# A channel mixer's first projection as seven half-size products per gate/up pair, from un-normalised sums, with the product kept in DRAM

## The chip, the cores and the metric

The kernel runs on one core of a Trainium2 chip, as one program in one launch. The metric is the device time of the launch in microseconds (us); a kernel's time is the median of its runs. A profiled execution is a single run with the hardware profiler; it gives the trace and its page.

## The reference, cut to what matters

One layer of a hybrid encoder works on 1056 frames of 1024 channels in float32: 1024 frames of a prompt and 32 of a sample stream, each group with its own modulation vectors. The token mixer (gated linear attention beside a short convolution) comes first, then the channel mixer:

```python
x = x + g1 * (merged @ w_o)                       # merged: 1024 channels
h = rmsnorm(x, norm2_g) * (1 + sc2) + sh2
gt, upv = jnp.split(h @ w_ffn_in, 2, axis=-1)     # 1024 -> 2 x 2816
x = x + g2 * ((jax.nn.silu(gt) * upv) @ w_ffn_out)
y = rmsnorm(x, norm_f_g)
```

## The kernel before, in words

Everything is kept transposed: channels on the 128 partitions, frames along the free axis. T = 1056 frames are cut into three blocks of 384, 384 and 288 columns (BO). A float32 product is three matmuls in the rounded format fp32r: every operand is split into a high part (a cast on ACT) and a low part (operand minus high part), and hi·hi, hi·lo and lo·hi are added up in PSUM (gemm_block). Weights come through load_w: one DMA of 512 KB on SP's queue into one of two raw buffers, a cast of 128x1024 on ACT, and a subtraction of 128x1024 on POOL.

The program is one list of steps, written in an order by hand; a scheduler then fixes each engine's instruction order, and each engine runs its list strictly in order. The stages are, by the trace:

- 0 to about 300 us: the first norm, the modulation vectors, q, k and v.
- to about 600 us: the attention, filled up with the projections of the convolution.
- to about 1010 us: output gate, merge gates, the attention's output projection.
- to about 1208 us: w_conv_out (loop over 8 weights, 3 blocks each), then w_o in three passes, one for each block, so that each of its 8 weights is loaded three times. The residual sum x1 stays in SBUF. Squares are summed on DVE (sq_acc), inv_rms turns them into 1/rms with a product with ones, a square root on ACT and RECIPROCAL on DVE, and norm2 writes the normalised, shifted and split operand h2.
- to the end: the channel mixer, in four parts of 5, 5, 6 and 6 of the 22 gate/up pairs (PARTS). For a pair, gemm2 takes for each block 24 matmuls of the gate's weight and 24 of the up weight, 144 in all; ev_gt applies silu on ACT, ev_up multiplies on DVE, and split makes the operand `a` of the second projection, its low part on POOL. After each part, w_ffn_out is applied to these `a` and added to x1 (add_gated).

A pair's inner work is thus this, once per block:

```python
gemm_block(psa, wa, acta, b, list(range(KT)))
t = eva(b, psa[:, : wd(b)])
psb = psm.tile([P, 512], F32, tag="m", name=nm("ps"))
gemm_block(psb, wb, actb, b, list(range(KT)))
evb(b, psb[:, : wd(b)], t)
```

Of the kernel before, what the change touches and what calls it, by code (L numbers as in the profile page):

```python
# [7 lines left out]
F32 = mybir.dt.float32  # L8
# [5 lines left out]
P = 128  # L14
# [18 lines left out]
PARTS = (5, 5, 6, 6)  # L33
# [24 lines left out]
def segs(b):  # L58
    lo, hi = BO[b], BO[b + 1]
    if hi <= S:  # L60
        return [(lo, hi, 0)]
    return [(lo, S, 0), (S, hi, 1)]
# [3 lines left out]
def hybrid_trunk(  # L66
# [117 lines left out]
    # ================= input norm, modulation, q/k/decay/v =================  # L184
    with tc.tile_pool(name="p1", bufs=1) as p1:
# [343 lines left out]
    # ================= gated linear attention, with the conv projections =================  # L529
    with tc.tile_pool(name="gl", bufs=1) as gl:  # L530
# [378 lines left out]
    # ================= merge, output projection, channel mixer =================  # L909
# [6 lines left out]
    def bt(b, tag, bufs=2):  # L916
        return r2.tile([P, BW], F32, tag=tag, name=nm(tag), bufs=bufs)[:, : wd(b)]

    og = []
    for j in range(KT):  # L920
        hi, lo = big(2 * j), big(2 * j + 1)
        og.append((hi, lo))

        def ev_g(b, ps, j=j, hi=hi, lo=lo):
            o = bt(b, "o")
            nc.sync.dma_start(o, o_d[:, j, blk(b)])
            sg = bt(b, "t")
            nc.scalar.activation(sg, ps, AF.Silu)
            nc.vector.tensor_tensor(sg, sg, o, op=ALU.mult)
            split(sg, hi[:, blk(b)], lo[:, blk(b)], "act", "dve")  # L930

        gemm(load_w(w_in[G0 + j]), h, ev_g)

    def gemm2(wa, acta, eva, wb, actb, evb, hook=None):
        for b in range(NB):
            if hook is not None and b == NB - 1:
                hook()
            psa = psm.tile([P, 512], F32, tag="m", name=nm("ps"))
            gemm_block(psa, wa, acta, b, list(range(KT)))
            t = eva(b, psa[:, : wd(b)])  # L940
            psb = psm.tile([P, 512], F32, tag="m", name=nm("ps"))
            gemm_block(psb, wb, actb, b, list(range(KT)))
            evb(b, psb[:, : wd(b)], t)

    for j in range(KT):

        def ev_ga(b, ps):
            sa = bt(b, "sa")
            nc.scalar.activation(sa, ps, AF.Sigmoid)
            return sa  # L950

        def ev_ya(b, ps, sa, j=j):
            nc.vector.tensor_tensor(sa, ps, sa, op=ALU.mult)
            nc.scalar.dma_start(mg_d[j][:, blk(b)], sa)

        gemm2(load_w(w_in[GA0 + j]), h, ev_ga, load_w(w_gla_out[j]), og, ev_ya)

    cpair = []
    for j in range(KT):

        def ev_gb(b, ps, j=j):
            sb = bt(b, "sa")
# [253 lines left out]
```

## Time and profile before

| | |
|---|---|
| time, median of 3 runs | 2021.74 us (2021.61 to 2021.79) |
| profiled execution: span, first to last instruction | 2017.7 us |
| PE (TensorE) busy, matmuls | 1928.9 us, 12121 |
| DVE (VectorE), ACT (ScalarE), POOL (GpSimd) busy | 863.2, 575.6, 728.9 us |
| mean granted TensorE clock | 0.984 of full speed |

Some 4 us of the time lie around the profile's span. Busy time is a union: back-to-back matmuls overlap, so a matmul's own duration is longer than the distance from its start to the next one's start, and it is this distance (called pitch below) that counts for a PE without gaps.

### The profile page before, as it was taken

The numbers are of one execution on the slowest core, as the hardware profiler recorded it, in microseconds if no ns is written. First come the engines' busy times: TensorE is split into PE (matmuls) and PEld (weight loads), VectorE is DVE, ScalarE is ACT, GpSimd is POOL, SyncE is SP. The second block draws the span as 40 slices with busy tenths as digits, with TensorE's granted clock in tenths as the row PEclk, the third lists the DMA queues.
The fourth block names the chain that finished last, engine by engine and source line by source line (L and its number), as shares of the span: only waits on it lengthen the run. The fifth ranks groups of instructions, "written<-read, shape, count | busy, mean of one in ns | idle before, by whom it ended". The sixth has DMA issues, their size and how long they took to land.

```text
span 2017.7 us, 29207 instructions
## 1 busy us (share of the span) xinstructions
PE 1928.9 (96%) x12121; PEld 1906.5 (94%) x12121; DVE 863.2 (43%) x1275; ACT 575.6 (29%) x940; POOL 728.9 (36%) x457
## 2 busy tenths in 40 slices
PE   6699988999999999999999998999999999999997
PEld 5699888998999999999999998999999999999997
DVE  7999958787773441000015688002002100110036
ACT  5333444444431231111312245211211111112122
POOL 5732247667542221222521353422322333223330
PEclk9799999999999999999999999999999999999999
DMA  7576843233212321222534453112111111111112
GB/s 273 174 278 212 275 126 108 76 104 94 77 61 74 108 90 63 66 83 87 164 102 142 137 168 99 53 34 62 43 41 44 54 52 35 47 46 42 55 40 87
DMA packets 102006, 200.56 MB, mean 99 GB/s; under 512 B 13457, under 2 KB 64785, under 8 KB 101874
## 3 DMA queue, kind: packets, MB, share of 16 engines
q1 hardware_dynamic: 73394, 165.26, 25.9%
q10 hardware_dynamic: 28480, 33.44, 4.7%
q8 instruction: 95, 1.56, 0.3%
q14 instruction: 37, 0.30, 0.0%
HBM read 165.15 MB, written 33.51 MB: 98 GB/s over the span
## 4 chain that ended last, share of the span: by engine, by line
PE 76%; DVE 12%; issue 4%; DMA 3%; POOL 2%; ACT 2%; SPq 1%; DVEq 0%; ACTq 0%; POOLq 0%
PE ps L132 71%; DVE junk L218 3%; PE pso L132 1%; POOL dt L740 1%; PE psv L132 1%; PE psk L132 1%; DMA wm<-in_w_modT 1%; DVE o L1043 1%; DVE td L444 1%; DVE h L349 1%; DVE tt L745 1%; DVE tt L744 0%; ACT whi L136 0%; PE psn L132 0%; PE pslv L132 0%
## 5 line engine op out<-in xcount | busy, mean ns | idle before, releaser
L140 POOL TENSOR_TENSOR wlo<-raw,whi 128x1024 fp32r<-128x1024 f32 (+2 forms) x170 | 397.4, 2339 | 718.9 <-ACT whi L136 703.6
L132 PE MATMUL ps<-h,whi 128*128 128x384 f32 (+2 forms) x2496 | 600.4, 325 | 6.6 <-DVE vst L511 4.0
L132 PE MATMUL ps<-g,whi 128*128 128x384 f32 (+1 forms) x2352 | 563.0, 325 | 0.0
L132 PEld LDWEIGHTS ps<-h,whi 128*128 128x128 f32 x2496 | 438.0, 190 | 7.5 <-ACT ta L435 4.2
L132 PEld LDWEIGHTS ps<-g,whi 128*128 128x128 f32 x2352 | 410.4, 188 | 0.3
L132 PE MATMUL ps<-h,wlo 128*128 128x384 f32 (+2 forms) x1248 | 405.6, 325 | 1.9 <-POOL wlo L140 1.9
L132 PE MATMUL ps<-g,wlo 128*128 128x384 f32 (+1 forms) x1176 | 380.0, 323 | 1.6 <-POOL wlo L140 1.6
L136 ACT CAST whi<-raw 128x1024 fp32r<-128x1024 f32 (+2 forms) x172 | 172.9, 1005 | 455.9 <-PE ps L132 398.5
L132 PEld LDWEIGHTS ps<-h,wlo 128*128 128x128 f32 x1248 | 236.0, 189 | 2.7 <-POOL wlo L140 2.1
L1100 DVE TENSOR_TENSOR sa<-ps,sa 128x384 f32<-128x384 f32 (+1 forms) x66 | 34.6, 524 | 456.7 <-PE ps L132 453.0
L132 PEld LDWEIGHTS ps<-g,wlo 128*128 128x128 f32 x1176 | 221.4, 188 | 1.9 <-POOL wlo L140 1.9
L132 PE MATMUL ps<-a,whi 128*128 128x384 f32 (+1 forms) x876 | 208.4, 323 | 0.0
L140 POOL TENSOR_TENSOR a<-sa,a 128x384 fp32r<-128x384 f32 (+1 forms) x66 | 62.6, 948 | 289.4 <-ACT a L136 289.4
L218 DVE CUSTOM_DVE_ANT_0 junk<-wm,cb 128x1024 f32<-128x1024 f32 x96 | 152.3, 1586 | 3.3 <-DMA wm<-in_w_modT 1.8
L132 PEld LDWEIGHTS ps<-a,whi 128*128 128x128 f32 x876 | 153.0, 188 | 0.3
L132 PE MATMUL ps<-a,wlo 128*128 128x384 f32 (+1 forms) x438 | 141.9, 324 | 0.0
L132 PE MATMUL ps<-hh,whi 128*128 128x384 f32 (+1 forms) x528 | 127.0, 323 | 2.9 <-DVE hh L1047 2.9
L992 DVE SCALAR_TENSOR_TENSOR x<-ps,mods,x 128x384 f32<-128x384 f32 (+2 forms) x128 | 59.9, 490 | 157.1 <-PE ps L132 157.1
L132 PE MATMUL psv<-vhi,h 128*128 128x256 f32 x512 | 98.8, 292 | 4.8 <-DVE vst L511 4.8
L132 PEld LDWEIGHTS ps<-hh,whi 128*128 128x128 f32 x528 | 91.9, 188 | 3.6 <-DVE hh L1047 3.6
L132 PEld LDWEIGHTS psv<-vhi,h 128*128 128x128 f32 x512 | 84.4, 200 | 5.0 <-DVE vst L511 5.0
L136 ACT CAST a<-sa 128x384 fp32r<-128x384 f32 (+1 forms) x66 | 32.1, 486 | 187.5 <-DVE sa L1100 187.5
(244 smaller groups left out, 2490.8 us busy)
## 6 DMA issues: line engine op xcount, KB each, us to landing
wm<-in_w_modT SPq DMA_DIRECT2D x64, 512.0 KB, 4.7
raw<-in_w_in SPq DMA_DIRECT2D x62, 512.0 KB, 3.5
raw<-in_w_ffn_in SPq DMA_DIRECT2D x44, 512.0 KB, 3.4
raw<-in_w_o SPq DMA_DIRECT2D x24, 512.0 KB, 3.4
raw<-in_w_ffn_out SPq DMA_DIRECT2D x16, 384.0 KB, 3.1
raw<-in_w_ffn_out SPq DMA_DIRECT2D x16, 320.0 KB, 2.9
x<-in_xT SPq DMA_DIRECT2D x8, 528.0 KB, 7.5
c_d<-ccs ACTq DMA_DIRECT2D x8, 528.0 KB, 2.7
```

Of the source, the lines that this page charges most:

```text
L132: nc.tensor.matmul(ps, lhsT, rhs, start=start, stop=stop)
L136: nc.scalar.copy(hi, raw)
L140: nc.gpsimd.tensor_tensor(lo, raw, f(hi), op=ALU.subtract)
L218: nc.vector.tensor_tensor_reduce(junk, wm, cb[:, st, :], 1.0, 0.0, ALU.mult, ALU.add, mods[:, st, j : j + 1])
L349: nc.vector.scalar_tensor_tensor(lo[:, :S], xp, shk, f(hi[:, :S]), op0=ALU.add, op1=ALU.subtract)
L444: nc.vector.tensor_tensor_scan(td[:, :S][:, ::-1], cm[:, :S], tb[:, :S][:, ::-1], 0.0, op0=ALU.mult, op1=ALU.add)
L740: nc.gpsimd.tensor_tensor(v3(Dt[:, ab]), src, ref, op=ALU.subtract)
L745: nc.vector.tensor_tensor(v4(Tt)[:, :, m:], v4(Tt)[:, :, m:], v4(Z1)[:, :, m:], op=ALU.mult)
L992: nc.vector.scalar_tensor_tensor(dst[:, lo:hi], ps[:, lo - BO[b] : hi - BO[b]], gate[s][:, j : j + 1], src[:, lo - src_off(src, b) : hi - ...
L1043: nc.vector.scalar_tensor_tensor(xr[:, sl], x1[k][:, a0:a1], am2[:, s, k : k + 1], r[:, sl], op0=ALU.mult, op1=ALU.mult)
L1100: nc.vector.tensor_tensor(sg, ps, sg, op=ALU.mult)
```

## The change

1. **First projection.** The weight of a gate/up pair is taken as a 2x2 matrix of blocks (gate or up column tile, by the lower or upper four of the eight channel tiles: x11, x12 for the gate, x21, x22 for the up half), the operand as a 2x2 matrix as well (lower or upper channel tiles, by the first or second 264 of 528 columns). The 2x2 product is made with seven products in Winograd's form. There are two column halves q, of 266 and 264 columns; the two extra columns carry the shift vectors, whose products become bias columns bz. A product is 4 channel tiles times three matmuls, so a pair has 2 x 7 x 12 = 168 matmuls.
2. **Operands.** The seven operand sums (ops; B11, B21, T2, T3, T1, B22, T4) are made once, during the output projection, from am2·x1, so without 1/rms and the shift (raw_op, prep, seven). 1/rms is kept as `rs` and multiplied in after the product (times_r).
3. **Weight sums.** For each pair DVE makes four sums s1 to s4 of 128x512, and each of the seven weight operands (granule) is split by a cast on ACT and a subtraction, five on DVE and two on POOL.
4. **Evacuation.** Three copies per column half on ACT take X out of PSUM between the products that go on accumulating in it; DVE adds W and V to them, multiplies by rs and gates.
5. **Product kept in DRAM.** The mixer's product goes to a_d, x1 to x1_d. After all 22 pairs x1 (8 loads of 528 KB) and the 22 rows of a_d are loaded again and split; the second projection has parts of 4, 6, 6 and 6.
6. **Output projections** run in four chunks of 264 columns; w_o in two passes, so 16 loads in place of 24. Squares are summed on POOL.
7. **Weight loads everywhere** come in two halves: two DMAs, two casts and two subtractions of 128x512, four raw buffers.

```diff
-PARTS = (5, 5, 6, 6)
+PARTS = (4, 6, 6, 6)
+CW = 264
...
-        load(raw, ap)
-        split(raw, hi, lo, hi_eng, lo_eng)
+        for k0, k1 in ((0, (nk + 1) // 2), ((nk + 1) // 2, nk)):
+            raw = raw_half(k1 - k0, w)
+            load(raw, ap[:, k0:k1, :])
+            split(raw, hi[:, k0:k1, :], lo[:, k0:k1, :], hi_eng, lo_eng)
...
+    def out_proj(j, w, c, first):
...
+        nc.scalar.dma_start(x1_d[j][:, ck(c)], x1)
...
+            nc.scalar.activation(q2, x1, AF.Square)
+            nc.gpsimd.tensor_tensor(ssq[c], ssq[c], q2, op=ALU.add)
...
+    def seven(q, ks, cols, b11, b12, b21, b22, t1, t2, t3_, t4_):
+        put(q, B11, ks, cols, b11)
+        put(q, B21, ks, cols, b21)
+        nc.vector.tensor_tensor(t1, b12, b11, op=ALU.subtract)
+        nc.vector.tensor_tensor(t2, b22, t1, op=ALU.subtract)
+        put(q, T2, ks, cols, t2)
+        put(q, T1, ks, cols, t1)
+        nc.vector.tensor_tensor(t3_, b22, b12, op=ALU.subtract)
+        put(q, T3, ks, cols, t3_)
+        put(q, B22, ks, cols, b22)
+        nc.vector.tensor_tensor(t4_, b21, t2, op=ALU.subtract)
+        put(q, T4, ks, cols, t4_)
...
+    def out_pass(q):
+        cs = (2 * q, 2 * q + 1)
+        for j in (0, 4, 1, 5, 2, 6, 3, 7):
+            w = load_w(w_o[j])
+            for c in cs:
+                out_proj(j, w, c, j == 0)
+                raw_op(j, c)
+                some_prep(2)
+            if j >= 4:
+                pend.append(prep(q, j - 4))
...
+        def fifth(q):
+            u4[q] = copy_of(X[q], q, 2)
+            a[q] = td()
+            add_to(a[q][:, CW:], V[q], q, u4[q], 3)
+            times_r(a[q][:, CW:], a[q][:, CW:], 2 * q + 1)
...
+        steps = [
+            (lambda: x11, nc.vector, X, B11, True, first),
+            (lambda: x12, nc.gpsimd, W, B21, True, second),
+            (lambda: wsum("s2", wsum("s1", x21, x22, ALU.add), x11, ALU.subtract), nc.vector, X, T2, False, third),
+            (lambda: wsum("s3", x11, x21, ALU.subtract), nc.vector, V, T3, True, None),
+            (lambda: sums["s1"], nc.vector, X, T1, False, fifth),
+            (lambda: wsum("s4", x12, sums["s2"], ALU.subtract), nc.vector, X, B22, False, sixth),
+            (lambda: x22, nc.gpsimd, V, T4, False, seventh),
+        ]
...
+    for fi in range(FT):
+        ffn_pair(fi)
...
+    for j in range(KT):
+        nc.sync.dma_start(x1[j], x1_d[j])
...
+            nc.sync.dma_start(raw, a_d[f0 + i])
+            hi, lo = unit(i, "r1" if final else "a"), unit(i, "r1")
+            split(raw, hi, lo, "act", "dve" if i % 2 else "pool")
```

How the change stands in the engines' lists is shown at three places. **First, DVE at the hand-over from the output projection to the channel mixer.** Before, these rows follow one another (sq is a block's sum of squares and its 1/rms, o and hh belong to norm2, sa to the first pair's evacuation):

```order
L1011 TENSOR_TENSOR sq_10853<-sq_10853,t_11118 128x288
L1047 SCALAR_TENSOR_TENSOR hh_10155<-o_11138,mods,hh_10154 128x384
L1020 RECIPROCAL sq_11123<-sq_11123 128x288
L1100 TENSOR_TENSOR sa_11181<-ps_11183,sa_11181 128x384
L1043 SCALAR_TENSOR_TENSOR o_11266<-x_1385_10156,am_120,sq_11123 128x256
L1043 SCALAR_TENSOR_TENSOR o_11266<-x_1385_10156,am_120,sq_11123 128x32
```

After the change these rows stand right behind the last two evacuations of the output projection (d_12161 is the last raw operand, the other small d are operand sums, op the split operands of the products; the d of 512 columns are weight sums s1, s2 and s3 of pair 0, rs is 1/rms):

```order
L1044 RECIPROCAL rs<-rs 128x264
L1075 TENSOR_TENSOR d_12203<-d_12161,d_12203 128x264
L1080 TENSOR_TENSOR d_12204<-d_12161,d_12067 128x264
L1187 TENSOR_TENSOR d_12276<-raw_12257,raw_12259 128x512
L1067 TENSOR_TENSOR op_11490<-d_12161,op_11489 128x264
L1084 TENSOR_TENSOR d_12204<-d_12161,d_12203 128x264
L1067 TENSOR_TENSOR op_11484<-d_12203,op_11483 128x264
L1067 TENSOR_TENSOR op_11486<-d_12204,op_11485 128x264
L1187 TENSOR_TENSOR d_12278<-d_12276,raw_12253 128x512
L1187 TENSOR_TENSOR d_12283<-raw_12253,raw_12257 128x512
L1044 RECIPROCAL rs<-rs 128x264
L1067 TENSOR_TENSOR op_11492<-d_12204,op_11491 128x264
```

The mixer's first products stood beside norm2's rows before; now the remaining operand sums, the first weight sums and both RECIPROCALs stand in one row ahead of the first weight operand that is made from a sum (a further eight rows on).

**Second, SP's DMA queue from the last pair to the second projection.** Before, the queue between a last pair's weights and the second projection held weights alone (raw):

```order
L153 DMA raw_14634<-in_w_ffn_in 128x1024
L153 DMA raw_14640<-in_w_ffn_in 128x1024
L153 DMA raw_14813<-in_w_ffn_in 128x1024
L153 DMA raw_14819<-in_w_ffn_in 128x1024
L153 DMA raw_14990<-in_w_ffn_out 128x768
L153 DMA raw_15057<-in_w_ffn_out 128x768
```

Now it holds these (a is a row of a_d, raw of in_w_ffn_in the block x22 of the last pair, x the residual sum, raw of in_w_ffn_out a half weight):

```order
L1323 DMA a_17857<-a_d_12231 128x1056
L154 DMA raw_17593<-in_w_ffn_in 128x512
L154 DMA raw_17883<-in_w_ffn_out 128x256
L154 DMA raw_17887<-in_w_ffn_out 128x256
L1280 DMA x_2320_17841<-x_d_10755 128x1056
L1280 DMA x_2321_17842<-x_d_10756 128x1056
L1280 DMA x_2322_17843<-x_d_10757 128x1056
L1280 DMA x_2323_17844<-x_d_10758 128x1056
L1323 DMA a_17863<-a_d_12232 128x1056
L154 DMA raw_17936<-in_w_ffn_out 128x256
L1280 DMA x_2324_17845<-x_d_10759 128x1056
L1280 DMA x_2325_17846<-x_d_10760 128x1056
L1323 DMA a_17869<-a_d_12233 128x1056
```

The first row of a_d went ahead of the last pair's x22, and four loads of x1 ahead of the second row of a_d, two more ahead of the third. By the same list, the load of the first row of a_d waits for PE to be done with the operand B11 of the last pair, and the first load of x1 for PE to be done with that pair's product T4.

**Third, ACT within a pair.** Before, a stretch in the second part reads (sa is the gate of a block, whi a weight):

```order
L1096 ACTIVATE sa_11829<-ps_11804 128x384
L136 CAST a_11735<-sa_11829 128x384
L136 CAST whi_11923<-raw_11922 128x1024
L1096 ACTIVATE sa_11884<-ps_11859 128x288
L136 CAST whi_12094<-raw_12093 128x640
L136 CAST a_11735<-sa_11884 128x288
L1096 ACTIVATE sa_11953<-ps_11928 128x384
L136 CAST a_11914<-sa_11953 128x384
```

After, a steady pair has these rows in a row (cp are the copies of X, psX the PSUM banks, wg the granules):

```order
L1205 ACTIVATE cp_17094<-cp_17094,bz_17093 128x264
L1205 ACTIVATE cp_17095<-cp_17095,bz_17093 128x264
L1193 COPY cp_17094<-psX_17087 128x266
L1193 COPY cp_17095<-psX_17088 128x264
L1157 CAST wg_17379<-raw_17335 128x512
L1193 COPY cp_17094<-psX_17087 128x266
L1193 COPY cp_17095<-psX_17088 128x264
L1157 CAST wg_17259<-d_17257 128x512
L1157 CAST wg_17350<-raw_17333 128x512
L1157 CAST wg_17417<-d_17415 128x512
L1157 CAST wg_17448<-d_17446 128x512
```

The copies that PE needs before it may accumulate on in X now stand behind silu rows, which need DVE's sums of W, and behind casts of weight sums, which DVE makes.

## Rows read from the trace of the kernel before

**Rows 1.** The page: the span, and part 1, busy time and instructions of each engine.

```profile
span 2017.7 us, 29207 instructions
PE 1928.9 (96%) x12121; PEld 1906.5 (94%) x12121; DVE 863.2 (43%) x1275; ACT 575.6 (29%) x940; POOL 728.9 (36%) x457
```

**Rows 2.** Windows: from:to us, length, busy of each engine, PEclk granted, DMA share, GB/s.

```profile
1200.00:1250.00 50.00, 43.84 (x280) 41.87 (x279) 44.72 (x58) 26.01 (x40) 25.75 (x12) 0.97 0.44 140
1208.00:1950.00 742.00, 736.56 (x4568) 734.85 (x4567) 132.07 (x247) 154.83 (x255) 232.38 (x146) 1.00 0.17 52
1950.00:2018.00 68.00, 56.87 (x354) 55.42 (x352) 41.53 (x72) 17.48 (x34) 4.83 (x4) 0.94 0.18 64
```

**Rows 3.** Timeline of PE in the output projection: start us, us, instruction.

```profile
1199.74 0.34 PE L132 MATMUL ps<-mhi,wlo 128*128 128x384 f32 x1
...
1202.02 0.29 PE L132 MATMUL ps<-mhi,whi 128*128 128x288 f32 x1
...
1203.48 0.30 PE L132 MATMUL ps<-mhi,wlo 128*128 128x288 f32 x1
```

**Rows 4.** Timeline of PE in the value projection, moving operand of 256 columns.

```profile
271.72 0.40 PE L132 MATMUL psv<-vhi,h 128*128 128x256 f32 x2
...
273.84 0.40 PE L132 MATMUL psv<-vhi,h 128*128 128x256 f32 x2
```

**Rows 5.** Groups by form: busy us, mean ns of one | idle before, releaser.

```profile
L992 DVE SCALAR_TENSOR_TENSOR x<-ps,mods,x 128x384 f32<-128x384 f32 x64 | 39.4, 616 | 117.2 <-PE ps L132 117.2
...
L992 DVE SCALAR_TENSOR_TENSOR x<-ps,mods,x 128x256 f32<-128x256 f32 x32 | 15.5, 484 | 39.9 <-PE ps L132 39.9
...
L1100 DVE TENSOR_TENSOR sa<-ps,sa 128x384 f32<-128x384 f32 x44 | 24.5, 557 | 330.2 <-PE ps L132 330.2
...
L1100 DVE TENSOR_TENSOR sa<-ps,sa 128x288 f32<-128x288 f32 x22 | 10.1, 458 | 126.5 <-PE ps L132 122.8 <-ACT sa L1096 3.7
...
L1020 DVE RECIPROCAL sq<-sq 128x384 f32<-128x384 f32 x4 | 10.2, 2544 | 1.9 <-ACT sq L1019 1.9
...
L136 ACT CAST whi<-raw 128x1024 fp32r<-128x1024 f32 x145 | 152.0, 1048 | 329.0 <-PE ps L132 271.5 <-issue 28.4 <-DMA raw<-in_w_in 15.5
...
L136 ACT CAST whi<-raw 128x640 fp32r<-128x640 f32 x16 | 11.7, 728 | 76.2 <-PE ps L132 76.2
...
L136 ACT CAST a<-sa 128x384 fp32r<-128x384 f32 x44 | 22.6, 514 | 187.5 <-DVE sa L1100 187.5
...
L140 POOL TENSOR_TENSOR wlo<-raw,whi 128x1024 fp32r<-128x1024 f32 x143 | 352.0, 2463 | 615.2 <-ACT whi L136 599.9 <-ACT bc L470 15.3
...
L140 POOL TENSOR_TENSOR wlo<-raw,whi 128x640 fp32r<-128x640 f32 x16 | 25.1, 1570 | 62.7 <-ACT whi L136 62.7
...
L140 POOL TENSOR_TENSOR a<-sa,a 128x384 fp32r<-128x384 f32 x44 | 44.8, 1019 | 289.4 <-ACT a L136 289.4
```

**Rows 6.** Timeline of POOL, then DVE, in the linear attention, around 562 us.

```profile
561.91 2.39 POOL L140 TENSOR_TENSOR wlo<-raw,whi 128x1024 fp32r<-128x1024 f32 x1
...
562.70 2.15 DVE L744 TENSOR_TENSOR tt<-tt,z 128x512 f32<-128x512 f32 x1 [0.37 <-ACT tt L741]
...
568.04 0.68 DVE L744 TENSOR_TENSOR tt<-tt,z 128x512 f32<-128x512 f32 x1
```

**Rows 7.** Windows, columns as above, after a pause of PE in the value projection.

```profile
258.00:261.00 3.00, 0.15 (x1) 0.15 (x1) 2.93 (x7) 0.00 (x0) 0.82 (x1) 0.60 0.41 139
261.00:264.00 3.00, 3.00 (x14) 3.00 (x15) 0.75 (x2) 2.79 (x3) 0.00 (x0) 0.50 0.21 74
264.00:267.00 3.00, 3.00 (x22) 3.00 (x22) 1.01 (x1) 2.53 (x4) 0.00 (x0) 0.76 0.00 0
```

**Rows 8.** The page, part 2 (GB/s in 40 slices) and part 6 (DMA issues).

```profile
GB/s 273 174 278 212 275 126 108 76 104 94 77 61 74 108 90 63 66 83 87 164 102 142 137 168 99 53 34 62 43 41 44 54 52 35 47 46 42 55 40 87
...
raw<-in_w_ffn_in SPq DMA_DIRECT2D x44, 512.0 KB, 3.4
...
c_d<-ccs ACTq DMA_DIRECT2D x8, 528.0 KB, 2.7
```

More of the change, by code (lines that the diff above doesn't have):

```diff
@@ L934, in gemm2 @@
[L934 to L956, printed above, removed]
@@ new lines, in out_proj, with inv_rms @@
+        nc.scalar.dma_start(x1_d[j][:, ck(c)], x1)
+        if first:
+            ssq[c] = te()
+            nc.scalar.activation(ssq[c], x1, AF.Square)
+        else:
+            q2 = te()
+            nc.scalar.activation(q2, x1, AF.Square)
+            nc.gpsimd.tensor_tensor(ssq[c], ssq[c], q2, op=ALU.add)
+    def inv_rms(ssqs, n, r):
+        ps = psx.tile([P, 512], F32, tag="x", name=nm("pss"))
+        for i, part in enumerate(ssqs):
+            mm(ps[:, :n], ones, part, i == 0, i == len(ssqs) - 1)
+        nc.scalar.activation(r, ps[:, :n], AF.Sqrt, bias=epst, scale=1.0 / D)
+        nc.vector.reciprocal(r, r)
+        return r
@@ new lines, in hybrid_trunk, with make_ops @@
+    B11, B21, B22, T4, T1, T2, T3 = range(7)
+    def make_ops(q):
+        n = 0
+        for i in (B11, B21, T2, T3, T1, B22, T4):
+            ops[q][i] = []
+            for _ in range(2):
+                sh = [P, 4, WQ[q]]
+                if q == 0 and n < 12:
+                    t = r2.tile(sh, F32R, tag="a", name=nm("op"), bufs=12)
+                elif q == 0 or n < 6:
+                    t = r2.tile(sh, F32R, tag="x", name=nm("op"), bufs=8)
+                else:
+                    t = r1.tile(sh, F32R, tag="r1", name=nm("op"))
+                ops[q][i].append(t)
+                n += 1
@@ new lines, in prep_shift, with quarter, some_prep @@
+    def prep_shift():
+        t = td().rearrange("p (i k n) -> p i k n", i=8, n=2)[:, :, :4, :]
+        def quarter(r, s):
+            return sh2[s][:, 4 * r : 4 * r + 4].rearrange("p (k n) -> p k n", n=1).to_broadcast([P, 4, 2])
+        b = [quarter(r, s) for r in range(2) for s in range(2)]
+        yield from seven(0, slice(0, 4), slice(CW, CW + 2), *b, *(t[:, i] for i in range(4)))
+    pend = []
+    def some_prep(n):
+        while pend and n > 0:
+            if next(pend[0], 0) == 0:
+                pend.pop(0)
+            n -= 1
@@ new lines, in hybrid_trunk, with granule @@
+    make_ops(1)
+    out_pass(1)
+    some_prep(99)
+    for c in (2, 3):
+        inv_rms([ssq[c]], CW, rs[:, ck(c)])
+    a_d = [dram.tile([P, T], F32, name=f"a_d{i}") for i in range(FT)]
+    gran = [0]
+    def granule(src, lo_eng):
+        gran[0] += 1
+        tag = ("whi", "wlo")[gran[0] % 2]
+        t = wp.tile([P, KT, P], F32R, tag=tag, name=nm("wg"), bufs=3)
+        hi, lo = t[:, :4, :], t[:, 4:, :]
+        nc.scalar.copy(hi, src)
+        lo_eng.tensor_tensor(lo, src, f(hi), op=ALU.subtract)
+        return hi, lo
```

350 lines of the change are left out of this document (227 added, 123 removed).

## The prediction

> **What bounds the kernel now.** I read the page first, then windows by stage, then PE's timeline for the pitch of a matmul, then the groups by form for what the other engines' operations cost, and last the pauses. PE is busy for 1928.9 of 2017.7 us [rows 1]. Windows show where the rest lies: from 1208 us to 1950 us, the channel mixer, PE is busy 736.56 of 742 us at a granted clock of 1.00, with DVE at 132, ACT at 155 and POOL at 232 us [rows 2]. So every matmul removed there shortens the run, as long as nothing else becomes late. Two places are not full: 1200 to 1250 us, the hand-over to the mixer, with 50.00 − 43.84 = 6.2 us of idle PE, and the tail after 1950 us with 11.1 us [rows 2]. Some 4 us of 2021.74 lie outside the span of the profiled execution; they stay. A change under 0.2% (4 us) can't be told from none here.
>
> **The pitch of a matmul.** Between the first two rows of [rows 3] lie 13 matmuls of 384 columns: 2.28 / 13 = 0.1754 us each. From the second to the third lie 11 of 288 columns: 1.46 / 11 = 0.1327 us. In the value projection 18 matmuls of 256 columns start in 2.12 us, 0.1178 us each, with a weight load for each [rows 4]. Per column that is 0.457, 0.461 and 0.460 ns, so there is no fixed part to pay at these sizes, and the line from 256 to 288 gives 0.1215 us for 264 columns and 0.1225 us for 266. The trace has no 264, but it has both neighbours.
>
> The Trainium skill speaks against the change here: in "TensorE: Matmul & The Clock Gate", section "Back-to-back issue gap", a sustained stream of weight loads and matmuls is put at about 81 ns for 128 columns and 131 ns for 512, so that halving the columns saves little. On a straight line between them (an estimate from that page) the 264 columns cost 99 ns and the 384 cost 114, and the first projection would go from 349 us to 365 us. The trace disagrees: 118 against 175 ns at 256 and 384 columns [rows 3, 4].
>
> **First projection.** Before: 22 pairs × 48 = 1056 matmuls in each block, 1056 × (2 × 0.1754 + 0.1327) = 510.6 us. After: 22 × 84 = 1848 in each column half, 1848 × (0.1225 + 0.1215) = 450.9 us. **−59.7 us.** Chunks of 264 in the two output projections: 2 × 8 × 24 = 384 matmuls in each chunk, 384 × 4 × 0.1215 = 186.6 against 384 × 0.4835 = 185.7 us, **+0.9**. The second projection keeps its matmuls.
>
> **Do the other engines keep up with a pair?** A pair is 168 matmuls, 20.5 us of PE. DVE gets, per pair, nine operations of 512 columns at 0.68 us [rows 6], 14 of two operands and 264 columns at 0.43 (0.557 at 384, 0.458 at 288 [rows 5]), four gates at 0.49 (0.616 and 0.484 [rows 5]) and six tiny ones, which I put at 0.2: 6.1 + 6.0 + 2.0 + 1.2 = 15.3 us. POOL's two subtractions of 512 columns, 1.27 us each on the line through 1024 and 640 [rows 5], can hold DVE up: in [rows 6] a DVE subtraction that starts during a POOL one takes 2.15 instead of 0.68 us and ends 0.55 us after it. So 15.3 + 2.5 = 17.8 of 20.5 us. ACT: seven casts of 0.62, six copies and five silus at 0.41 or less (1.048, 0.728 and 0.514 us at 1024, 640 and 384 [rows 5]), 8.9 us. On sums, PE stays the bound. On order it is tight: in the list of ACT the third copy of X stands behind silu, which waits for two DVE steps on W; walking a pair with these durations the copy is ready some 2 us before PE wants X again. I cost this at nothing; what covers it is those 2 us.
>
> **Hand-over to the mixer.** After the last out-projection matmul DVE must still do the row shown with the change: two RECIPROCALs of 2.544 × 264 / 384 = 1.75 us [rows 5], seven operand sums and splits, three weight sums, and so on. The first RECIPROCAL waits for the sums of squares, which stand behind 24 mixer matmuls (2.9 us) and need a product with ones and a square root (some 1.1 us, an estimate), to about 4.0 us; then 1.75 + 6 × 0.43 + 2 × 0.68 us and a cast of 0.62 make the first high weight part ready at 10.3 us, and the low part, after the second RECIPROCAL, at 14.6 us. PE has 4.8 us of work to the first and 2.1 us between: idle 7.7 us. **A pause has an aftermath:** at 258 to 261 us PE did nearly nothing; after it the granted clock was 0.50 (its level of 1.2 GHz, against 2.4) and PE got through 14 and 22 matmuls in two windows of 3 us that hold 25 each at full clock [rows 7]. That is 14 too few, 14 × 0.118 = 1.7 us lost, 2 us with the end of the pause. So 7.7 + 2 against 6.2 before: **+3.5** (0 if preparation is done earlier, +9 if POOL holds DVE up).
>
> **Output projection.** A pass is 46.8 us of PE. DVE has four preparations of 11 operations and 16 scalings, at most 60 × 0.43 = 25.8 us, beside 16 additions out of PSUM. POOL has 16 subtractions at 1.27 and 14 additions of squares at 0.73 (1.019 at 384 [rows 5]): 30.5 us. If they exclude each other wholly, 56.3 us, 9.5 too many per pass, +19 in all; if overlap and the backlog take it up, nothing. I take a quarter, **+5**, since work left over may trail into the next stage.
>
> The Trainium skill has this as a rule: in "SBUF — State Buffer", section "Who interferes with whom", a VectorE operation with two SBUF inputs and a GpSimd one that reads SBUF lock each other out for a whole instruction. [rows 6] agree (0.55 us after POOL's end), and by the rule alone the +19 would stand.
>
> **Last pair.** x22 of this pair stands behind the first row of a_d on SP's queue, and that load waits until PE is done with B11. Then 528 KB (2.7 us alone [rows 8]) and 256 KB land by about 4.2 us (at 270 GB/s, the page's best slices [rows 8], plus issue and latency), three weight sums (2.0 us) and the low parts (1.4) follow: 7.6 us, of which PE covers some 2 with the rest of B11, leaving about 6, and 2 of aftermath: **+8** (4 to 10).
>
> **Second projection's start.** The first load of x1 waits for product T4 of the last pair; row 1 of a_d stands behind four loads of x1, so 2.7 MB pass first: 10 us at 270 GB/s, 1 of issue and latency (528 KB alone take 2.7 us where that rate makes 2.0 [rows 8]), 2 for the cast and the subtraction; PE has 2.5 us of work meanwhile: 10.5 idle, 2 of aftermath. Row 3 of a_d stands behind four more x1, one more row and four half weights: 3.8 MB or 14 us, against 8.2 us of matmuls: 5.5. **+18** (10 to 24). Later rows of a_d are fetched parts ahead; their casts, 1.1 us, lie beside matmuls.
>
> **Halved loads.** A weight's subtraction becomes 2 × 1.27 in place of 2.46 us [rows 5], and holds DVE half as long at a time. Where PE is full this hides. In the first 600 us either sign is possible, ±6; I take 0.
>
> **Sum.** −59.7 + 0.9 + 3.5 + 5 + 8 + 18 = −24.3; 2021.7 − 24.3 = 1997.4 us, or a span of 1993.
>
> **The rivals.**
> - *Hand-overs hidden.* If loads and sums come early enough that only 6.2 us at each border remain, the time is 2021.7 − 58.8 + 6 to 16, so 1969 to 1979. For: DMA is far from full in the mixer, 0.17 [rows 2]. Against: x1's slots are really held by operands until the end. 0.12.
> - *A pair bound by its chain* (the other side). Place: the third copy on ACT, behind silu, behind DVE. If the chain runs over the 2 us slack, each of 22 pairs is longer; at 1.1 us per pair the gain of 24 us is gone; at 2 it is 1997 + 44 = 2041, at 3 it is 2063. For: DVE needs 17.8 of 20.5 us and strict order; signals between engines aren't in my sums. Against: a pair's product needs none of it until its last steps. 0.16.
> - *A matmul at 264 columns doesn't get shorter in proportion.* Then the first projection adds 16 us rather than taking 60: 2073. It needs a fixed part that 256 columns don't show [rows 4]. 0.02.
> - *The costs cancel the gain.* +19 in the output projection, +9, +10 and +24 at the borders give 2022 − 58.8 + 62 = 2025: no change. 0.06.
>
> **How the numbers follow.** My own case, PE-bound pairs with costly borders, has 0.64 and spans 1980 to 2016. Faster by over 0.2%: it and the first rival, and a little of the chain running over by under 0.9 us: 0.78. Same: 0.07. Slower: 0.15. The range leaves out the best part of the first rival and the worse part of the chain: 1971 to 2028.
>
> **What would show it.** Right: a pitch of 0.121 to 0.123 us in the mixer, 453 us of it, windows there with PE at 100% and clock 1.00; three pauses, 8, 6 and 10 us, each followed by a window at 0.50, the first ended by a granule's subtraction on DVE, the second by x22, the third by row 1 of a_d. Wrong: PE below 95% in the middle of the mixer with waits on the copies of X or on granules; or matmul pitch above 0.13; or an output projection well over 94 us.

## The result, and the profile after

The changed kernel takes **1969.55 us** (median of 4 runs, 1968.82 to 1970.61) against 2021.67 us: a ratio of 0.9746, 95% interval 0.9732 to 0.976. That is 52 us faster, just below the range of 1971 to 2028 and 27 us below the 1997 forecast. The profiled execution has a span of 1967.2 us, 50.5 us shorter than before. The kernel before took 2018 to 2022 us (medians), depending on the chip, so below every kernel is compared by its ratio to the kernel before on its own chip, and stages by their places in the profiles.

The page after, span and part 1; it answers to [rows 1]:

```profile
span 1967.2 us, 33099 instructions
PE 1879.8 (96%) x13035; PEld 1856.0 (94%) x13035; DVE 1106.9 (56%) x2007; ACT 680.9 (35%) x1354; POOL 709.1 (36%) x554
```

PE has 914 matmuls more and is busy for 49 us less. Almost the whole gain is PE's work; its idle time stayed at 87 to 89 us. Windows by stage, with the columns of [rows 2]: the output projection, the hand-over, the middle of the mixer, the last pair's end, and the start of the second projection in pieces of 4 us:

```profile
1128.20:1235.60 107.40, 99.88 (x795) 97.59 (x794) 87.02 (x175) 49.32 (x124) 62.19 (x56) 0.98 0.49 148
1235.60:1252.00 16.40, 12.78 (x81) 11.71 (x81) 13.78 (x25) 9.33 (x19) 2.51 (x3) 0.80 0.23 74
...
1300.00:1650.00 350.00, 350.00 (x2851) 350.00 (x2850) 231.79 (x542) 138.54 (x306) 44.11 (x34) 1.00 0.24 78
1672.00:1692.00 20.00, 20.00 (x162) 20.00 (x161) 14.23 (x30) 9.42 (x21) 6.14 (x5) 1.00 0.68 237
```

```profile
1688.00:1692.00 4.00, 4.00 (x31) 4.00 (x31) 2.46 (x6) 2.08 (x4) 0.24 (x1) 1.00 1.04 412
1692.00:1696.00 4.00, 3.51 (x25) 2.96 (x24) 3.96 (x9) 0.21 (x1) 1.27 (x1) 1.00 1.04 410
1696.00:1700.00 4.00, 3.65 (x25) 3.33 (x24) 2.74 (x4) 2.39 (x5) 2.75 (x2) 1.00 0.73 272
1700.00:1704.00 4.00, 2.10 (x10) 1.78 (x10) 1.81 (x3) 1.68 (x3) 2.00 (x3) 0.87 0.52 182
1704.00:1708.00 4.00, 4.00 (x18) 3.82 (x18) 2.80 (x6) 0.20 (x1) 0.00 (x0) 0.70 0.89 305
```

In the mixer PE is full at a granted clock of 1.00, and DVE's 231.79 of 350 us are 66%. PE is full through the last pair as well (1672 to 1692 us). The pause that was forecast at 10.5 us for the second projection's start is a few short ones between 1692 and 1704 us, 2.74 us in all, with a window at 0.70 behind them.

The length of a pair is read from POOL, whose subtraction of L1158 comes at the same place of every pair. Its timeline, start and duration, in the first and in the eighteenth of such pairs:

```profile
1307.64 1.31 POOL L1158 TENSOR_TENSOR wg<-raw,wg 128x512 fp32r<-128x512 f32 x1 [14.91 <-ACT wg L1157]
...
1658.64 1.29 POOL L1158 TENSOR_TENSOR wg<-raw,wg 128x512 fp32r<-128x512 f32 x1 [14.91 <-ACT wg L1157]
```

Seventeen pairs lie between them: 351.00 / 17 = 20.647 us a pair, or 0.1229 us for each of its 168 matmuls. The forecast, read from 256 and 288 columns [rows 3, 4], was 20.5 us and 0.122. In the list of waits from 1120 to 1300 us one sees what PE waited for at the hand-over; the columns are who waits, for whom, us in total, times, longest:

```profile
PE pss L133 <- POOL e L1037: 4.4, 3, 1.9
PE ps L133 <- DVE e L1027: 2.9, 4, 0.9
PE psX L1165 <- DVE e L1027: 2.1, 1, 2.1
PE psV L1165 <- ACT wg L1157: 0.7, 1, 0.7
```

The same places in PE's timeline (idle time before the row, and its releaser, in brackets):

```profile
1230.67 1.97 PE L1165 MATMUL psX<-op,wg 128*128 128x264 f32 x12 [2.14 <-DVE e L1027]
1234.49 1.25 PE L133 MATMUL pss<-e,ones 128*128 128x264 f32 x2 [1.85 <-POOL e L1037]
1237.65 1.25 PE L133 MATMUL pss<-e,ones 128*128 128x264 f32 x2 [1.91 <-POOL e L1037]
1238.32 3.23 PE L1165 MATMUL psW<-op,wg 128*128 128x266 f32 x12
```

So the hand-over's pauses are ended by the last evacuations (L1027) and by the sums of squares on POOL (L1037), and the product at 1238.32 takes 3.23 us for 12 matmuls, where a full clock gives 12 × 0.123 = 1.5. The forecast had the first pause ended by a granule's low part on DVE; none of the long ones is.

**Where the 50.5 us of span came from.** Each row is the length of a stretch between the same instructions in both profiles, or a term read from the rows above:

| term | forecast | measured |
|---|---|---|
| front: start to the first silu of the output gate (674.4, now 667.9 us) | 0 (±6) | −6.5 |
| output gate to the end of w_conv_out | – | 0.0 |
| output projection and hand-over, with chunks, lock and hand-over (+0.9, +5, +3.5) | +9.4 | +1.5 and +6.4 |
| first projection, 22 × 20.647 against 510.6 us | −59.7 | −56.4 |
| last pair | +8 | 0 |
| second projection's start | +18 | +4.5 |
| tail | 0 | −0.1 |

The +1.5 is the stretch from the last sum of w_conv_out to the last evacuation of w_o: 107.5 us, 1127.9 to 1235.4, against 106.0 from 1134.4 to 1240.4 before. The +6.4 is the start of the mixer: 3.62 idle in the second window above, and 2.8 for matmuls at a low clock (12.78 us busy, where 81 × 0.123 = 10.0 would do). The first projection's row takes the prediction's sum of 510.6 us for the kernel before. The +4.5 is 2.74 idle and 1.8 for the low clock. The rows add up to −50.6. From the last evacuation of w_o to the last of the second projection the profiles have 720.4 us against 765.7, −45.3, where the rows of this part add up to −45.5. Some 2 us of the time's gain lie outside the span; what they are is open. In the repeats on another chip (below) both kernels take some 2 us outside their spans, and the gain is 49 us, so these 2 us are not shown to belong to the change.

SP's queue at the last pair shows why the forecast borders didn't come (start, duration of the issue, line, transfer):

```profile
1668.73 0.33 SPq L1323 DMA_DIRECT2D a<-a_d  x1
1669.15 0.38 SPq L154 DMA_DIRECT2D raw<-in_w_ffn_in  x1
...
1678.40 1.81 SPq L1280 DMA_DIRECT2D x<-x_d  x4
1680.26 0.58 SPq L1323 DMA_DIRECT2D a<-a_d  x1
...
1683.13 2.28 SPq L1280 DMA_DIRECT2D x<-x_d  x2
1688.81 0.32 SPq L1323 DMA_DIRECT2D a<-a_d  x1
...
1690.10 0.79 SPq L1280 DMA_DIRECT2D x<-x_d  x2
1690.99 2.82 SPq L154 DMA_DIRECT2D raw<-in_w_ffn_out  x3
1694.71 0.33 SPq L1323 DMA_DIRECT2D a<-a_d  x1
```

Beside it PE's timeline and, from the list of waits of SP's queue from 1640 to 1712 us, its longest wait for PE, and the one wait of a load of x1 for a product into V:

```profile
1667.18 2.25 PE L1165 MATMUL psW<-op,wg 128*128 128x266 f32 x17
...
1672.71 5.56 PE L1165 MATMUL psX<-op,wg 128*128 128x266 f32 x44
...
1688.53 3.14 PE L1165 MATMUL psV<-op,wg 128*128 128x266 f32 x24
```

```profile
SPq L1323 <- PE psW L1165: 8.5, 1, 8.5
...
SPq L1280 <- PE psV L1165: 0.3, 1, 0.3
```

The first row of a_d goes out when the first 12 matmuls of W, the product with B21, are done (1667.18 + 12 × 0.123 = 1668.7). PE makes this product of the last pair ahead of the one with B11, whose first half ends inside the 5.56 us row, at some 1676.6 us. And of the eight loads of x1 only the last two wait for T4, a product into V, whose first half ends at 1690.0: four go out from 1678.40 on, ten microseconds before T4's product starts, two more from 1683.13 on.

**So the words on B11 and T4 ahead of the prediction, below the rows of SP's queue, are wrong.** The list of rows names only the engine that a load waits for. The engine, PE, was read there; which product it is was put in from the order in which the operands were made, as if the first load got the last operand's buffer.

### The profile page after: what moved, and what is told of

Same layout as the page of the kernel before. It is cut to its first block, busy times and chain, and to the rows that moved or that the text cites. A ratio compares the mean times of both kernels' runs of the same rounds, so it can differ in the third digit from the quotient of the medians.

```text
span 1967.2 us, 33099 instructions
## 1 busy us (share of the span) xinstructions
PE 1879.8 (96%) x13035; PEld 1856.0 (94%) x13035; DVE 1106.9 (56%) x2007; ACT 680.9 (35%) x1354; POOL 709.1 (36%) x554
## 4 chain that ended last, share of the span: by engine, by line
PE 66%; DVE 3%; DMA 1%; issue 1%; ACT 1%; POOL 1%; ACTq 0%; DVEq 0%; SPq 0%; POOLq 0%
PE ps L133 43%; PE psX L1165 12%; PE psV L1165 6%; PE psW L1165 3%; DVE op L1067 1%; PE pso L133 0%; DMA a_d<-d 0%; DMA a<-a_d 0%; POOL wlo L141 0%; DMA e<-in_xT 0%; DVE e L1027 0%; DVE d L1187 0%; PE pslv L133 0%; PE pss L133 0%; DMA raw<-in_w_ffn_in 0%
## 5 line engine op out<-in xcount | busy, mean ns | idle before, releaser
L141 POOL TENSOR_TENSOR wlo<-raw,whi 128x512 fp32r<-128x512 f32 (+2 forms) x236 | 320.6, 1378 | 582.0 <-ACT whi L137 520.3
L1165 PE MATMUL psX<-op,wg 128*128 128x266 f32 (+1 forms) x2112 | 274.6, 286 | 3.6 <-DVE e L1027 2.1
L1165 PEld LDWEIGHTS psX<-op,wg 128*128 128x128 f32 x2112 | 265.9, 189 | 4.8 <-issue 2.3
L137 ACT CAST whi<-raw 128x512 fp32r<-128x512 f32 (+2 forms) x240 | 129.7, 585 | 287.5 <-PE ps L133 160.8
L1158 POOL TENSOR_TENSOR wg<-raw,wg 128x512 fp32r<-128x512 f32 x44 | 57.2, 1301 | 376.8 <-ACT wg L1157 332.1
L133 PE MATMUL ps<-g,whi 128*128 128x264 f32 (+2 forms) x896 | 185.0, 301 | 0.0
L133 PEld LDWEIGHTS ps<-g,whi 128*128 128x128 f32 x896 | 146.2, 188 | 0.0
L1165 PE MATMUL psV<-op,wg 128*128 128x266 f32 (+1 forms) x1056 | 144.9, 286 | 0.7 <-ACT wg L1157 0.7
L1165 PEld LDWEIGHTS psV<-op,wg 128*128 128x128 f32 x1056 | 136.0, 189 | 1.0 <-ACT wg L1157 1.0
L133 PE MATMUL ps<-g,wlo 128*128 128x264 f32 (+2 forms) x448 | 134.8, 301 | 0.0
```

Source lines behind the costliest of these rows:

```text
L133: nc.tensor.matmul(ps, lhsT, rhs, start=start, stop=stop)
L137: nc.scalar.copy(hi, raw)
L141: nc.gpsimd.tensor_tensor(lo, raw, f(hi), op=ALU.subtract)
L1158: lo_eng.tensor_tensor(lo, src, f(hi), op=ALU.subtract)
L1165: nc.tensor.matmul(ps, l[:, k, :], r[:, k, :], start=first and k == 0 and i == 0, stop=k == 3 and i == 2, skip_group_check=True,)
```

## The experiments

### The halved loads alone

The theory: the front's 6 us come from the weight loads in two halves and nothing else. Edit, in the kernel before (the value projection's weights, which have a loop of their own, are halved in the same way):

```diff
-        load(raw, ap)
-        split(raw, hi, lo, hi_eng, lo_eng)
+        for k0, k1 in ((0, (nk + 1) // 2), ((nk + 1) // 2, nk)):
+            raw = raw_half(k1 - k0, w)
+            load(raw, ap[:, k0:k1, :])
+            split(raw, hi[:, k0:k1, :], lo[:, k0:k1, :], hi_eng, lo_eng)
```

> The kernel before with one part of the change alone: weights come in two halves (two DMAs, two casts, two subtractions of 128x512, four raw buffers). The comparison of the two traces has the first silu of the output gate 6.5 us earlier after the change, and only the halved loads touch the code ahead of it. Theory: the halves are worth these 6.5 us by themselves, because POOL's subtractions hold DVE half as long and operands start earlier; the run takes 2015 us, with the first silu of the output gate near 668 us in place of 674. Rival: the 6.5 us come from something else that shifts in the first 600 us when the later code changes (the scheduler's order, where buffers lie); then 2021 us, and the silu at 674.

Measured: 2011.66 against 2017.98 us, ratio 0.9971 (0.996 to 0.9982), so −6 us. The first silu of the output gate starts at 668.8 us, where it is 674.4 before and 667.9 after. Windows of this kernel, and below them of the kernel before:

```profile
0.00:100.00 100.00, 67.33 (x303) 59.76 (x304) 87.94 (x114) 45.61 (x58) 69.39 (x39) 0.88 0.64 229
100.00:200.00 100.00, 94.11 (x680) 92.75 (x679) 96.96 (x143) 38.02 (x74) 48.77 (x32) 0.98 0.72 251
```

```profile
0.00:100.00 100.00, 64.51 (x298) 56.38 (x299) 89.34 (x110) 44.86 (x51) 63.13 (x35) 0.90 0.63 223
100.00:200.00 100.00, 92.92 (x650) 91.96 (x650) 96.26 (x142) 35.83 (x62) 32.71 (x23) 0.95 0.73 249
```

What follows: halving alone gives the front's gain, 5.6 of the 6.5 us; in the two other profiles of the changed kernel the silu starts at 669.1 and 669.9 us, so the two can't be told apart. Of it, 4.0 us more of PE's work are done by 200 us; PE's wait for the first norm's cast, 11.3 us before, is 6.1 here. Which of the halved operations brings this forward was not taken apart. In this profile the output projection's stretch is shorter as well, 103.6 us in place of 106.0, so the +1.5 in the table may hold a gain from the halves beside the new costs there.

### When the loads of x1 and a_d go out

Two kernels move the loads. In the first, x1 is loaded behind four more rows of a_d; in the second, rows and x1 go out as the prediction had assumed, x1 only after T4's product. Edits, the first kernel's and then the second's main lines (last_a and last_v hold V of the last pair's first column half):

```diff
     for j in range(KT):
+        if j == 0:
+            nc.vector.tensor_copy(x1[j][:, 0:1], last_a[0][:, 0:1])
         nc.sync.dma_start(x1[j], x1_d[j])
```

```diff
-    for j in range(KT):
-        nc.sync.dma_start(x1[j], x1_d[j])
+    def load_x1(*js):
+        for j in js:
+            if j == 0:
+                nc.vector.tensor_copy(x1[j][:, 0:1], last_v[0][:, 0:1])
+            tc.keep_in_program_order(nc.sync.dma_start(x1[j], x1_d[j]))
...
+            if part == 0 and i > 0:
+                load_x1(*((0, 1, 2, 3), (4, 5), (6, 7))[i - 1])
```

> The changed kernel, with the loads of the residual sum x1 behind the first rows of the mixer's product in SP's queue (the first x1 also waits for the last pair's product T4). Theory: of the time that the second projection's start costs now, the wait for row 3 (1.9 us of idle PE, and two windows of 4 us with a granted clock of 0.87 and 0.70) comes from six loads of x1 that pass ahead of it; with them behind, PE doesn't wait and the run is 2 to 4 us shorter, 1966 to 1968 us. Rival: the rows are held up by the cast and subtraction chain or by the free slots and not by the queue; then no change, 1969 to 1970 us.

> The changed kernel, made to do what the prediction assumed: the first load of x1 waits until PE is done with the last pair's product T4 on the first column half, and the loads of x1 and of rows 1 to 3 keep the order x1 x1 x1 x1, row 1, x1 x1, row 2, x1 x1, row 3. In the changed kernel these loads are issued from 1678.4 us on, 10 us before that product starts. Theory: the release was the step that failed, and the transfers run at the 410 GB/s that the changed kernel's trace shows and not at 270; then 5 loads take 6.6 us, the stall is about 7 us at row 1 and 2 at row 3, with 2 to 3 us of low clock, and the run takes 7 to 8 us longer than the changed kernel, 1977 us. Rival 1: the release alone, at 270 GB/s, as predicted: 14 us longer, 1983 us. Rival 2: the release didn't matter, since the loads would be hidden anyway: 1970 us.

Measured, x1 behind a_d: 1966.38 us, ratio 0.9747 (0.9733 to 0.9762), not to be told from the change by the ratio. Locally it is: from the last granule on POOL to the first evacuation of the second projection pass 21.1 us, against 24.8 (24.8, 23.5 and 23.8 us in three profiles of the changed kernel). PE's longest wait at the border is 0.7 us.

Measured, x1 after T4: 1979.29 us, ratio 0.9815 (0.9799 to 0.9832); the same stretch is 34.5 us, 9.7 longer than after the change. Its waits from 1680 to 1780 us and its windows:

```profile
PE ps L133 <- ACT a L137: 8.2, 2, 5.7
```

```profile
1696.00:1700.00 4.00, 0.14 (x1) 0.00 (x0) 0.52 (x2) 0.03 (x1) 0.00 (x0) 1.00 1.03 397
1700.00:1704.00 4.00, 2.16 (x7) 2.00 (x8) 1.26 (x1) 1.07 (x1) 0.00 (x0) 0.53 0.99 362
1704.00:1708.00 4.00, 1.90 (x7) 1.40 (x5) 0.00 (x0) 1.13 (x2) 0.73 (x1) 0.50 1.06 412
1708.00:1712.00 4.00, 2.67 (x7) 2.24 (x8) 0.00 (x0) 0.64 (x2) 2.42 (x1) 0.50 1.03 409
```

What follows: PE now waits for rows of a_d behind x1, the pause that the prediction had described. When the loads go out is worth some 10 of the 13.5 us by which that term was too large. For the rest there is the rate, 362 to 412 GB/s, where 270 had been read from slices of 50 us [rows 8]: PE's waits are 9.1 us, where 10.5 + 5.5 = 16 had been forecast. No run changes the rate alone, so this part is argued. The pauses cost more than their idle time: in the 12 us from 1700 the clock is at 0.50 to 0.53, where 0.50 is its level of 1.2 GHz.

### Is the pair's length PE's alone?

The theory: in the mixer nothing but PE counts. One kernel leaves product T4 out; two others give DVE 10 and 16 more operations of 264 columns for each pair, in the chain from W to the gate. Edits:

```diff
-            product(dst[q], w, ops[q][i], start)
+            if i != T4:
+                product(dst[q], w, ops[q][i], start)
```

```diff
         def third(q):
+            for _ in range(5):
+                nc.vector.tensor_tensor(p1[q][:, C], p1[q][:, C], p1[q][:, C], op=ALU.max)
             u2[q] = copy_of(X[q], q, 1)
```

> The changed kernel without the matmuls of one of the seven products (T4), all other work left in: the output then lacks that product. A pair has 144 matmuls and 17.7 us of PE in place of 20.65. It asks how far the other engines are from being the bound. Theory: a pair is bound by PE and the others have room, so each pair gets 2.95 us shorter, 22 x 2.95 = 65 us, 1905 us, with windows in the mixer still at 100% PE. Rival: DVE (13.65 us busy per pair by the windows) and its order leave only some 2 us of slack, as the prediction had it; then a pair stops at about 18.6 us, the gain is 45 us, 1925 us, and PE waits for granules or copies of X.

> The changed kernel with ten more operations of two SBUF operands and 264 columns per pair on DVE, in the gate's chain (each takes the maximum of a tile with itself, so nothing changes in value); 0.34 us each in a row, 3.4 us per pair. It asks how much of a pair DVE's row still has free. Theory: DVE is busy for 231.79 us in 350 us of the mixer, 13.7 us of a pair's 20.65; with 3.4 it has 17.1, and with 2.5 us of waits behind POOL 19.6, so PE stays the bound and the run stays at 0.975 of the kernel before, 1966 to 1971 us. Rival: the third copy of X stands behind this chain with some 2 us of room, as the prediction had it; then each pair gets 1.4 us longer and the run 31 us, near 2000 us.

> The same with sixteen such operations, 5.5 us per pair. Theory: 13.7 + 5.5 = 19.2 us of DVE per pair, with up to 2.5 us of waits behind POOL 21.7; this is about where DVE takes over from PE, so a pair takes 20.65 to 21.7 us and the run 1969 to 1993 us. Rival, with 2 us of room ahead of the third copy: 3.5 us per pair, 77 us, near 2046 us.

Measured without T4: 1908.87 us, the ratio to its chip's kernel before being 0.9459 from a single run. A pair takes 17.634 us (between POOL's rows of L1158 at 1304.02 and 1603.80 us lie 17 pairs, 299.78 / 17), 3.01 less than 20.647, and 24 × 0.123 = 2.95 was taken out. PE stays full:

```profile
1200.00:1250.00 50.00, 39.32 (x273) 37.51 (x273) 41.18 (x88) 22.44 (x56) 21.72 (x21) 0.90 0.40 131
...
1300.00:1600.00 300.00, 300.00 (x2452) 300.00 (x2451) 216.96 (x545) 134.88 (x307) 44.16 (x34) 1.00 0.27 91
1600.00:1650.00 50.00, 45.40 (x332) 44.52 (x331) 36.49 (x75) 24.62 (x51) 18.46 (x14) 0.97 0.66 225
```

The whole is 60 us of span rather than 22 × 3.01 = 66 shorter. This run's first silu starts 2.4 us later (670.3 us), and the pauses at the borders are a little longer: 12.0 us idle from 1128 to 1252 us and 4.6 from 1600 to 1650, against 11.1 and 2.7 at the same places after the change.

Measured with more DVE work: 1970.12 us with 10 operations (changed kernel on the same chip 1969.88), 1983.52 with 16. Windows of the one and the other, and the other's longest wait there:

```profile
1300.00:1650.00 350.00, 350.00 (x2850) 350.00 (x2849) 310.35 (x713) 137.91 (x306) 47.31 (x34) 1.00 0.23 79
```

```profile
1300.00:1650.00 350.00, 343.01 (x2760) 339.37 (x2759) 326.10 (x784) 131.82 (x296) 47.47 (x32) 1.00 0.22 76
```

```profile
PE psV L1165 <- DVE bz L1215: 6.7, 15, 0.7
```

What follows: ten operations cost nothing, with DVE at 310.35 of 350 us (89%). It is busy for 78.56 us more there than after the change, 4.6 us a pair. At 93% PE waits for DVE's reading of V, 6.7 us in the 350 and at most 0.7 at a time. So the room in a pair is at least 4.6 us, not the 2 us of the walk through ACT's list, and the rival of a pair bound by its chain has no ground in this kernel.

### The sums of squares on DVE, and the RECIPROCALs later

Two kernels ask what the output projection and the hand-over cost. One moves the sums of squares from POOL to DVE; the other makes the last two 1/rms behind the fourth granule of the first pair:

```diff
-            nc.gpsimd.tensor_tensor(ssq[c], ssq[c], q2, op=ALU.add)
+            nc.vector.tensor_tensor(ssq[c], ssq[c], q2, op=ALU.add)
```

```diff
-    for c in (2, 3):
-        inv_rms([ssq[c]], CW, rs[:, ck(c)])
...
+            if n == 3:
+                for c in (2, 3):
+                    inv_rms([ssq[c]], CW, rs[:, ck(c)], pinned=True)
```

> The changed kernel with the sums of squares of the output projection on DVE, as the kernel before had them, and not on POOL. It takes 28 operations of 0.75 us from POOL and gives DVE 28 of 0.43 us. Theory: the prediction's term for the lock between DVE and POOL in the output projection (+5 us, 19 at most) was too large because DVE, 73 of 100 us busy there, has room, and its splits take 0.71 instead of 0.43 us without PE waiting for them; so the move changes the passes little, and PE's wait for the sums of squares at the hand-over (4.4 us behind POOL's additions in the changed kernel) is given back in part to a longer row on DVE: within 2 us of the changed kernel, 0.9740 to 0.9752. Rival: the lock does cost what was predicted; without POOL's additions the passes get 3 to 5 us shorter, 0.9725.

> The changed kernel, with the two RECIPROCALs that make 1/rms of the last two chunks moved behind the first weight operands in DVE's list. In the changed kernel PE loses 9.2 us at the hand-over to the mixer and then runs at 0.50 of its clock for some 6 us; between the last evacuation and the first low part of a weight sum DVE spends 3.6 us on these RECIPROCALs. Theory: the hand-over is bound by DVE's row, as predicted, so taking 3.6 us out of it shortens the pause by 2 to 3.5 us and the run by as much, 0.9730 of the kernel before. Rival: the row is bound by what it waits for (the sums of squares behind POOL's additions, the casts on ACT), or 1/rms is then late for the silu on which the copies of X wait; no change, 0.9746, or 1 us longer.

> The changed kernel once more, unaltered, beside the three runs that follow, since chips differ by some microseconds and a change of a few is to be read from one chip. Expected: 0.9746 of the kernel before.

Measured: the sums on DVE 1967.36 us, ratio 0.9739 (0.9721 to 0.9758); the later RECIPROCALs 1967.35, 0.9739 (0.9721 to 0.9756); the changed kernel beside them 1970.07, 0.9754 (0.9739 to 0.9769). The ratios can't tell them apart. The stretches can, that of the RECIPROCALs barely. From the first to the last evacuation of the output projection pass 101.2 us with the sums on DVE, and 104.6, 104.3 and 104.0 in three profiles of the changed kernel. From there to the last granule on POOL pass 444.2 us with the sums on DVE and 444.0 with the later RECIPROCALs, against 445.4, 445.6 and 445.1. The operand splits of this stretch, by form (count, busy us, mean ns), from 1120 to 1260 us, of the changed kernel and of the one with the sums on DVE:

```profile
L1067 DVE TENSOR_TENSOR op<-d,op 128x264 fp32r<-128x264 f32 x56 | 38.7, 711 | 10.8 <-ACT op L1066 10.7
```

```profile
L1067 DVE TENSOR_TENSOR op<-d,op 128x264 fp32r<-128x264 f32 x56 | 26.1, 486 | 0.6
```

What follows: with 28 fewer operations on POOL the same DVE subtraction takes 486 instead of 711 ns, and the passes are some 3 us shorter though DVE has 28 operations more, as the rival of this run had it. (In the next section's kernel with three edits they take 102.1 us; kernels with the sums on POOL have 103.2 at the least.) That the lock between DVE and POOL is the way fits the 711 ns, but the edit also takes the sums out of POOL's row, and no run parts the two. PE's wait for these sums isn't shorter: 5.6 us with them on DVE, 4.4 and 5.4 in two profiles of the changed kernel. The two RECIPROCALs, 3.45 us of DVE, cost about 1 us where they stood: profiles with the same mixer and without this edit have 444.8 to 445.6 us, this one 444.0.

### The three together

> The changed kernel with two edits together: the RECIPROCALs late, and the loads of x1 behind the first rows of the mixer's product. Theory: the two act at places 450 us apart, so their gains add: 3 us from the first and 3 us from the second, 0.9716 of the kernel before, a version faster than both. Rival: neither place is what bounds there: 0.9746.

> The changed kernel with three edits together: squares summed on DVE, the RECIPROCALs late, the loads of x1 behind the first rows of the mixer's product. In the profiles of the runs with one of them, the output projection's passes take 101.2 us in place of 104.6 with the first, the stretch from the last evacuation of the output projection to the last subtraction of the last pair is 1.2 to 1.4 us shorter with the first or the second, and the stretch from there to the second projection's first addition 3.7 us shorter with the third. Theory: they act at three places, so they add to some 8 us: 0.971 of the kernel before, 1961 to 1963 us. Rival: what is gained in one place is waited for in the next (the sums of squares on DVE lengthen the row that the late RECIPROCALs shorten); then 4 us, 0.9735.

> The changed kernel unaltered, as the yardstick for the run with three edits on the same chip. Expected: 0.975 of the kernel before.

x1 behind a_d and the later RECIPROCALs alone: 1966.23 us, ratio 0.9735 (0.9719 to 0.9751). Locally they give some 2.1 us at the later RECIPROCALs and 3.5 at the loads, but in its profile the front ended later than in any other with the same code (the first silu at 672.6 us; 667.7 to 671.0 elsewhere). The 0.9716 that was expected lies just below the interval; the total alone says little. With the sums of squares on DVE as third edit: **1960.22 us** (1959.37 to 1962.77), ratio 0.9711 (0.9698 to 0.9724), against 1969.88 and 0.9756 (0.9743 to 0.977) for the changed kernel on the same chip. The intervals don't touch: this version beats both kernels. Its windows at the two borders:

```profile
1120.00:1250.00 130.00, 121.88 (x964) 119.72 (x964) 107.56 (x241) 61.66 (x149) 44.77 (x31) 0.99 0.43 138
...
1650.00:1710.00 60.00, 59.17 (x440) 58.56 (x439) 42.05 (x82) 25.98 (x54) 22.21 (x17) 1.00 0.60 215
```

The second border has 0.83 us of idle PE left. At the first, 8.1 us remain, of which the list of waits puts 4.5 to the sums of squares, now on DVE.

## Why the prediction missed

- **What bounds the kernel, and the pitch: right.** The mixer was PE's before and is PE's after. The step from 256 and 288 columns to 264 held within 1%, 0.1229 against 0.122 us. On a pair the difference is 0.15 us, on 22 pairs it is the 3.3 us by which −59.7 was too much. The Trainium skill, in "TensorE: Matmul & The Clock Gate", section "Back-to-back issue gap", would give an estimate of 99 ns for a matmul of 264 columns; this stream of fp32r products shows 122.9, and the measurement decides.
- **The other engines keep up: right, the slack too small.** The forecast had DVE at 15.3 us a pair, 17.8 with POOL's locks. The windows show 231.79 / 350 × 20.647 = 13.7. The room is at least 4.6 us, as the ten added operations show. The chance of 0.16 on a pair bound by its chain came from walking a list without asking how far ahead PE's work lies.
- **Output projection, hand-over and chunks: right in sum, wrong in what ends the pauses.** +9.4 was forecast, +7.9 measured, and part of that nearness may be luck: the 2.4 us that the kernel with halves alone gains in the same stretch weren't in the sum. PE's products with w_o run from 1127.7 to 1227.0 us, 99.3 us, where their matmuls alone were put at 93.6, so the +5 by itself was well sized. PE waits for the last evacuations and for the sums of squares on POOL. Moving these sums is worth 2 to 3.4 us in the passes and up to 1.2 behind them, where +5 was forecast for the lock. The Trainium skill, in "SBUF — State Buffer", section "Who interferes with whom", says that VectorE and GpSimd exclude each other on their shared port; 711 against 486 ns for one and the same operation agree. The +19 that the prediction put for full exclusion did not come.
- **Last pair: the step that failed first.** "That load waits until PE is done with B11": it waits for B21, and PE makes the product with B21 some 8 us before it has done the first half of B11. The row of a_d and x22 went out at 1668.73 and 1669.15, and PE had work until they were there. +8 became 0.
- **Second projection's start: the step that failed most.** "The first load of x1 waits for product T4": six of eight loads went out before T4's first half was done, as the buffers of B11, B21 and T2 came free. The kernel that really waits for T4 has the pause, 9.1 us in three waits, so the mechanism was sound and its release wrong. The rate was wrong too, 410 GB/s in full windows where 270 was taken. +18 became +4.5.
- **Halved loads: a wrong zero.** ±6 was the bound. The first silu came 6.5 us earlier in the first profile, and 5.3 and 4.5 us in two later ones; the halves alone give 5.6.
- **The rival that came** is that of hidden hand-overs, 1969 to 1979 us, with 0.12. Its counter-argument, that x1's slots are held by operands until the end, holds for two of the eight. Its borders, put at 6 to 16 us, measured 7.9 + 4.5 = 12.4; that the time came out at its lower end is due to the front's −6.5 and the 2 us outside the span, which its sum did not have.

## What to carry to other kernels

An order list says which engine a load waits for, not which instruction. Where a term of the sum hangs on the release of a buffer, find in the list the last user of each buffer that could be given to it, and cost the earliest and the latest; here they lay 10 us apart. And when products are reordered by a scheduler, take the place of a product from PE's list, not from the source.

Read a transfer rate from the stretch in which the queue is full, not from slices of the whole run. And where GpSimd and DVE work side by side before a border, look at what the border waits for and at how long DVE's operations take there: moving one small sum off GpSimd gave 2 to 4 us.

## What the runs showed of the hardware

- One core's queue moved 410 and 412 GB/s in windows of 4 us, with the DMA share at 1.04; slices of the page show 285 at most. The Trainium skill, in "DMA: Bandwidth & Descriptors", section "Where 436 GB/s comes from", puts the limit of the fabric at 435, which these windows come near to. The same section has the memory's side, about 358 for each core, as the bound of transfers from memory into SBUF; these loads passed it for 8 us, so here the measurement decides.
- After a pause a matmul of 384 columns started 0.32 us behind the last one, against 0.17 at full clock (in the kernel with x1 after T4, 1703.62 to 1704.26 us). There the granted clock stayed at 0.50 to 0.53 (0.50 is its level of 1.2 GHz) through 12 us in which PE was busy for 6.7 us between short pauses; after the change a pause of 1.90 us was followed by one window of 4 us at 0.70.
- With DVE busy for 89% of the mixer, its added work inside the chain of the gate, PE did not wait at all; at 93% it waited 6.7 us in 350.
